# Key norms and T's products ahead of the Gram products, wider scan gaps, and later constants, adds and loads in the first layer

## The chip, the cores and the metric

The kernel runs on one core of a Trainium2 chip. The metric is the device time of one execution in microseconds (us). TensorE (PE) does the matrix products, VectorE (DVE), ScalarE (ACT) and GpSimd (POOL) the elementwise work, and SyncE (SP), ACT and POOL issue DMAs from their instruction queues. Each queue runs in the order in which it was written.

## The reference, cut to what matters

Two residual layers on x of 512 tokens by 2048 channels, all in float32.

```
layer 0: out = diff_attention(rms_norm(x)), 8 heads, w_in 2048 x 8192, w_out 2048 x 2048
         a = softmax(q1 k1) - lam * softmax(q2 k2);  o = rms_norm(a v) * silu(gate);  x += o @ w_out
layer 1: out = rwkv7(rms_norm(x)), 32 heads of 64, w_in 2048 x (4*2048 + 192), w_out 2048 x 2048
         p = token-shifted h @ w_in -> r, k, v, g, and decay w, rate a from a low-rank part
         kk = k / max(|k|, 1e-12) per head
         scan over t:  S = S * w_t + (S a_t) b_t + v_t k_t,   y_t = S r_t     (a = -kk, b = kk * a)
         y = group_norm(y) ... * silu(g);  x += y @ w_out
```

The scan of layer 1 is done in chunks of 64 tokens: the Gram products of the keys and receptances within a chunk, an inverse T of a triangular matrix made from them and from the key norms |k|, and then a short chain of small products from chunk to chunk.

## The kernel before, in words

**Precision and projections.** A float32 operand is split into a rounded high part and the rest (`split_w`: ACT casts `wh` on L105, DVE subtracts for `wl` on L106), and a product is three matmuls, high by high, high by low, low by high (`mm3`). A weight group of 512 KB (tile `wraw`) is loaded, split by ACT and DVE, and used by 128x512 matmuls. All these projections are the main stream of PE (tile `pp`, L122 and L567).

**Chains.** Work that isn't a projection is threaded into this stream by hand. `Chain` is a generator whose `yield n` says after how many more projection matmuls its next step is issued. `tick` is called after each projection matmul and counts down the *first* chain of the list only; the next chain begins to count when the first has ended. `finish` issues all remaining steps of a chain at once. `issue_after` and `high_priority` set what an instruction is ordered behind within its queue.

**First layer.** Eight heads, one after the other; `unit_head` (L540 on) makes q, k, v and gate of a head with sums of halves of the weights: three of four weight blocks are loaded, used, and then changed in place by an accumulating DMA that POOL issues (`add_w`, L86), in tiles `Ta` to `Td` and `wraw`. Head h's projections carry the attention of head h-1 as a chain (start 56 ticks in, 20 for head 1). In the `h == 1` turn the constants of the second layer (`rwkv_consts`: three DMAs on ACT, then on DVE 2 + 10 + 8 small operations, L1164 to L1171, from tile `pb`) are made as a chain with `yield 10` and `yield 8`; as it was appended before the attention chain of head 1 is, that chain stands behind it. In the last head, `third()` loads the weights of block (2,2) (`b22`) with the load ordered behind the last matmul of product S2, and the add straight behind the load. After the heads, rows `hH`, `hL` of the attention output are read back by SP (L931), and `new_x` (L945) loads x for the residual: column blocks 0 and 1 from POOL's queue, 2 and 3 from SP's.

**Second layer.** A loop over 16 pairs of heads, j = 0 to 15. One turn has four projections (k, r, v, gate) of 48 matmuls each, 192 ticks. In turn j:

- `chain(j-1)` is begun: `t_combine` loads the inverse's blocks into `TT`, waits 10 ticks, transposes on DVE (`T1`, L1382; a profile row calls it T), waits 8, makes T's products (tile `px`, L1388), waits 19, the second products (L1398), waits 8; then `scan_pair`, eight chunks of three steps: `sm<-VS,G` (L1469), `sm<-rhs,TT` (L1480), `sm<-VS,BKT` (L1487), with `gap` ticks after the first and second and `gap_s` after the third. Between them ACT copies `rhs` (L1472) and `VS` (L1482), and DVE makes the next `VS` (L1491). Gaps are (6, 7) at j = 3 and (6, 8) for j = 4 to 14. After the last chunk come the outputs `Y` (L1509 and L1513, both buffers of PSUM bank `pc`) and `centre` on DVE (L1524 to L1526), which frees them.
- 18 ticks into the v projection, `behind` finishes the chain of pair j-2, if it hasn't ended, and issues `gram(j)`: 32 Gram products `gp` (L1290; first half in bank `pb`, second half in bank `pc`), and right behind them one step of the running chain, T's products. Then come four ACT copies to `G`, the key norms (two `pt<-sHx` / `pt<-sLx` matmuls, L1209 and L1210, in bank `pb`), the ACT copy `ssl` (L1302), and DMAs on SP that write norms (`ltd<-ssl`) and Gram blocks (`ltd<-G`, L1310) to DRAM.
- `t_solve` reads them back (`LT<-ltd`, four DMAs on POOL, L1344) and solves for T on DVE (`tmpl`, `Tm`, L1346 to L1358). The result goes through DRAM to the next turn's `TT`.

Of the kernel before, what the change touches and what calls it, by code (L numbers as in the profile page):

```python
# [13 lines left out]
F32 = mybir.dt.float32  # L14
# [9 lines left out]
P = 128  # L24
D = 2048
T = 512
# [56 lines left out]
def add_w(g, raw, part, k0):  # L83

    w, c = part
    g.nc.gpsimd.dma_start(out=raw[:], in_=w[c][:, k0 : k0 + KG], accum_op=ALU.add)  # L86


@urgent
# [441 lines left out]
def unit_head(g, aps, h, t1s, sq, turned):  # L531


    nc = g.nc
    c1, c2 = qk_cols(aps, h), vg_cols(aps, h)
    acc1 = g.work.tile([P, 2, 512], F32, name="acc1", tag="acc1", bufs=1)
    acc = [None, None, acc1[:, 0], acc1[:, 1]]
    q = [t[:] for t in t1s]
    N = NH4 // KG
    last = h == NH - 1  # L540

    def pair():
        return [g.pp.tile([P, 512], F32, name="pp", tag="pp") for _ in range(2)]

    def load(i, k0, parts):
        pool, tag, bufs = (g.work, "Te", 1) if i == N - 1 else (g.wraw, "wraw", 3)
        raw = pool.tile([P, KG, 512], F32, name="wraw", tag=tag, bufs=bufs)
        load_w(g, raw, parts, k0 + i * KG, slice(0, KG))
        return raw

    def split(raw):
        return split_w(g, None, KG, 512, 0, raw)

    def block(k0, t0):
        return lambda k, t: [x[k0 + k][:, t0 + t * P : t0 + (t + 1) * P] for x in (g.hH, g.hL)]

    def form(nm, i):
        return lambda k, t: [x[:, t * P : (t + 1) * P] for x in g.sums[nm][i * KG + k]]

    def products(out, lhs, raw, start=False, end=False):  # L560
        wt = split(raw)
        for t in range(2):
            first = start
            for lo in range(2):
                for k in range(KG):
                    for x in lhs(k, t)[: 2 - lo]:
                        m = nc.tensor.matmul(out[t][:], x, wt[lo][:, k, :], start=first, stop=end and lo == 1 and k == KG - 1,  # L567
                                             skip_group_check=True)
                        tick(g, m)
                        first = False  # L570

    def all_groups(out, lhs, raw, start=False, end=False, then=None):
        for i in range(N):
            r = raw(i)
            products(out, lhs(i), r, start and i == 0, end and i == N - 1)
            if then:
                add_w(g, r, then[0], then[1] + i * KG)

    def s4(out, keep, start=False, end=False):
        def raw(i):  # L580
            keep.append(load(i, NH4, c2))
            return keep[-1]
        all_groups(out, lambda i: form("S4", i), raw, start, end, None if last else (c2, 0))

    chained = lambda i: g.Ts[i]
    y = pair()
    all_groups(y, lambda i: block(NH4 + i * KG, 0), lambda i: load(i, NH4, c1), True, True)
    copy_out(g, q[:2], y)
    y = pair()
    all_groups(y, lambda i: block(i * KG, 0), chained, True, False, (c2, 0))  # L590
    take(g, q[:2], y)
    X = pair()
    all_groups(X, lambda i: form("S1", i), chained, True, last, (c2, NH4))
    copy_out(g, acc[2:], X)
    b22 = []
    if not last:
        s4(X, b22, end=True)
        G, acc[:2] = gates(g)
        copy_out(g, acc[:2], X)
    all_groups(y, lambda i: form("S2", i), chained, then=(c1, NH4))  # L600
    behind = g.m.ins
    if last:
        G, acc[:2] = gates(g)
    take(g, acc[:2], y, ALU.subtract, acc[2:] if last else None)

    def square():
        X = pair()
        all_groups(X, lambda i: block(NH4 + i * KG, 256), chained, True, True)
        return X

    def third():
        for i in range(N):
            if last:
                with g.tc.issue_after(behind):
                    b22.append(load(i, NH4, c2))
                add_w(g, b22[i], c2, i * KG)
            products(y, form("S3", i), b22[i], end=i == N - 1)
        take(g, acc[2:], y, ALU.subtract)

    head_qk(g, t1s, sq, [0, 1])  # L620
    if last:
        copy_out(g, q[2:], square())
        third()
        take(g, q[2:], y)
        head_qk(g, t1s, sq, [2, 3])
        turned()
        X = pair()
        s4(X, [], True, True)
        take(g, acc[:2], X)
        return head_vg(g, h, acc, G)  # L630
    turned()
    third()
    copy_out(g, q[2:], y)
    values = head_vg(g, h, acc, G)
    X = square()
    first_tiles(g, aps, h + 1)
    take(g, q[2:], X)
    head_qk(g, t1s, sq, [2, 3])
    return values
# [156 lines left out]
def layer0(g, aps):  # L796
# [3 lines left out]
    with ExitStack() as cx:  # L800
# [91 lines left out]
        for h in range(NH):  # L892
# [11 lines left out]

            rest = [(g, t1s, *qkT, t) for t in (2, 3)]
            if h:
                values = unit_head(g, aps, h, t1s, sq, lambda: Chain(g, keys(2), 9))
            else:
                for ts in ([0, 1], [2, 3]):
                    head_qk(g, t1s, sq, ts)  # L910
                Chain(g, keys(2), 120)
                input_sums(g, pairs, False)
                ps = unit_tok(g, g.hH, g.hL, vg_cols(aps, h), 512)
                acc1 = g.work.tile([P, 2, 512], F32, name="acc1", tag="acc1", bufs=1)
                G, vg = gates(g)
                vg += [acc1[:, 0], acc1[:, 1]]
                copy_out(g, vg, ps)
                for c in list(g.chains):
                    c.finish(g)
                input_sums(g, pairs, True)  # L920
                first_tiles(g, aps, 1)
                values = head_vg(g, h, vg, G)
            before = qkT + (sq,) + values
            if h == 1:
                Chain(g, rwkv_consts(g, aps))
                g.chains[0].step(g)
        rows = []
        for k in range(KT - 2):
            rows.append([g.hp.tile([P, T], F32R, name=n, tag=n) for n in ("hH", "hL")])
            for x, d in zip(rows[k], g.ys):  # L930
                nc.sync.dma_start(out=x[:].bitcast(F32), in_=d[k * P : (k + 1) * P, :])  # L931
        ch = Chain(g, attention(g, h, *before, 20, rows, rest), 16)

        def all_rows(n, _):
# [6 lines left out]

        def new_x(cb):
            xq = g.work.tile([P, NT, 512], F32, name="xq", tag=("sA", "sB", "qkL", "qkT")[cb], bufs=1)
            for t in range(NT):
                (nc.gpsimd if cb < 2 else nc.sync).dma_start(out=xq[:, t, :], in_=aps["x"][0, t * P : (t + 1) * P, cb * 512 : cb * 512 + 512])  # L945
            xs.append(xq)
            return xq

# [330 lines left out]
def gram(g, j, p, before):  # L1279

    nc, w, BK = g.nc, g.work, p.BK
    p.G = w.tile([P, NC_, 2, 2, C], F32, name="G1", tag="G1", bufs=2)
    p.BKT = w.tile([P, NC_, P], F32, name="BKT", tag="BKT", bufs=2)
    halves = []
# [10 lines left out]
    for c0, gp in halves:  # L1295
        for h in range(2):
            nc.scalar.copy(p.G[:, c0 : c0 + 4, :, h, :], gp[h][:].rearrange("p (u x t) -> p u x t", u=4, x=2))
    ps = g.ps.tile([P, 512], F32, name="pt", tag="pb", bufs=2)
    sum_channels(g, ps[:2, :], g.ones[:, 0 : P : C], p.k2)
    ss = w.tile([2, T], F32, name="ssl", tag="thg", bufs=1)  # L1300
    with g.tc.high_priority(offset=SOLVE if j == D // P - 1 else 0):
        nc.scalar.copy(ss[:], ps[:2, :])  # L1302
        for half in range(2):
            nc.sync.dma_start(
                out=g.ltd[j % 2, half, :, :, HALF, :],
                in_=ss[:].rearrange("h (c b t) -> h c b t", c=NC_, b=2)[:, :, half, :])
        for half in range(2):
            for h in range(2):
                q0 = h * C + half * HALF
# [53 lines left out]
GAP_D, GAP_X, GAP_T = 18, 19, 8  # L1363


def t_combine(g, j, p):

    nc, w, TT = g.nc, g.work, g.TT[j % 2]
    for h in range(2):
# [5 lines left out]
    T1 = w.tile([P, NC_, HALF], F32, name="T1", tag="T1", bufs=1)  # L1375
    X = w.tile([P, NC_, HALF], F32, name="X", tag="X", bufs=1)
    px = g.ps.tile([P, 512], F32, name="px", tag="pd", bufs=1)
    yield GAP_D - GAP_T
    for h in range(2):
        r_ = slice(h * C, h * C + C)  # L1380
        with g.tc.issue_after(g.centred) if g.centred else ExitStack():
# [64 lines left out]
HEADS = ((0, slice(0, C)), (1, slice(C, P)))  # L1446


def chain(g, j, p, delay, gap, gap_s, others=()):
    def steps():  # L1450
        yield from t_combine(g, j, p)
        yield from scan_pair(g, j, p, gap, gap_s, dict(others))

    p.chain = Chain(g, steps(), delay)
    return p.chain
# [97 lines left out]
def layer1(g, aps):  # L1553
    nc, tc = g.nc, g.tc
    with ExitStack() as cx:
# [22 lines left out]
        for j in range(D // P):  # L1578
            p = pairs[j]
            if j:  # L1580
# [2 lines left out]
                if j > 1:  # L1583
                    others.append((3, lambda i=j - 2: finish_y(g, i, pairs[i])))
                full = LAG <= j < D // P - 1
                gaps = (6, 8 if j > LAG else 7) if full else (4, 5) if j > 1 else (3, 4)
                chain(g, j - 1, pairs[j - 1], 5, *gaps, others).step(g)
                if j == 1:
                    pairs[0].chain.wait += 34
            stage2(g, j, r, p)  # L1590

            def behind(m, j=j, p=p):
                if j > 1:
                    pairs[j - 2].chain.finish(g)
                with tc.issue_after(m.ins):
                    gram(g, j, p, j > 2 and pairs[j - 1].chain)
                p.rfs = split_act(g, p.rf[:], w, "x")
                if j == 2:
                    pairs[1].chain.wait = 16
# [160 lines left out]
```

## Time and profile before

| what | us |
|---|---|
| median of 3 runs | 2133.65 (2128.92 to 2135.13) |
| the profiled execution | 2131.0 |
| its span in the trace | 2129.3 |
| PE busy in the span | 2091.2 |
| one turn of the second layer, start of `gp` to start of `gp` (1379.27 to 1441.18) | 61.91 |

All stretches below are in us from the start of the span. A row of the time line has the start, the duration, the engine and line, the operation with its output and inputs, and in brackets the idle time of the engine before it with what ended that. A row of the windows has, for one stretch, its length, the busy time of PE, PE's weight loads, DVE, ACT and POOL with numbers of instructions, then the TensorE clock that was granted, as a share of full speed, the busy share of the DMA engines and GB/s. Rows of the waits have total, number and longest.

### The profile page before, as it was taken

The page shows a single profiled execution, that of the slowest core. Times are in us where ns is not written, and L with a number is a line of the kernel's source. Part 1 is how long each engine was busy: PE and PEld are TensorE (multiplying, and loading weights), DVE is VectorE, ACT ScalarE, POOL GpSimd, SP SyncE. Part 2 cuts the span into 40 slices and gives each one's busy share as a digit, 9 for nine tenths or more (in the row PEclk, how much of TensorE's full clock was granted, in tenths as well). Part 3 has the DMA queues.
Part 4 walks back from the last instruction along what each step waited for, and adds up shares of the span by engine and source line. Part 5 has one row for each costly group of instructions (what it writes and reads, how often), then busy time and mean ns, then how long its engine had stood idle before and what let it go on. Part 6 is the DMA issues. An engine that isn't in the chain of part 4 may idle for free.

```text
span 2129.3 us, 34082 instructions
## 1 busy us (share of the span) xinstructions
PE 2091.2 (98%) x11852; PEld 1690.3 (79%) x11852; DVE 1613.0 (76%) x4129; ACT 1155.5 (54%) x2278; POOL 367.9 (17%) x735
## 2 busy tenths in 40 slices
PE   9999999999999999999999999999999999999999
PEld 7888788888887788878677877778777777877787
DVE  6987888888888875576677777887777788776645
ACT  5765556566565543355555555555555555545322
POOL 1021111102113000101222221222222122231101
PEclk9999999999999999999999999999999999999999
DMA  8587878879789936722222332332333333345565
GB/s 266 161 166 186 161 167 186 164 189 172 178 183 215 314 113 179 150 90 88 78 74 84 98 91 84 93 91 77 94 103 88 84 91 92 107 134 178 173 171 121
DMA packets 158972, 294.60 MB, mean 138 GB/s; under 512 B 64352, under 2 KB 81760, under 8 KB 158800
## 3 DMA queue, kind: packets, MB, share of 16 engines
q1 hardware_dynamic: 109696, 182.82, 27.7%
q0 software_dynamic: 24448, 85.64, 22.0%
q10 hardware_dynamic: 24656, 23.97, 3.4%
q8 instruction: 93, 1.52, 0.3%
q14 instruction: 79, 0.65, 0.1%
HBM read 268.71 MB, written 23.66 MB: 137 GB/s over the span
## 4 chain that ended last, share of the span: by engine, by line
PE 77%; DVE 10%; ACT 6%; issue 3%; DMA 3%; ACTq 0%; POOL 0%; SPq 0%; DVEq 0%; POOLq 0%
PE pp L122 36%; PE pp L567 21%; PE pt L122 4%; DVE wl L106 3%; ACT wh L105 1%; PE gp L1290 1%; PE sc L122 1%; PE sm L1480 1%; PE sm L1469 1%; PE sm L1487 1%; PE o L122 1%; DVE tmpl L1355 1%; ACT VS L1427 1%; PE lora L122 1%; PE z L122 1%
## 5 line engine op out<-in xcount | busy, mean ns | idle before, releaser
L106 DVE TENSOR_TENSOR wl<-wraw,wh 128x1024 fp32r<-128x1024 f32 (+2 forms) x291 | 360.4, 1239 | 257.5 <-ACT wh L105 249.7
L105 ACT CAST wh<-wraw 128x1024 fp32r<-128x1024 f32 (+2 forms) x291 | 303.8, 1044 | 296.9 <-PE pp L122 130.3
L122 PE MATMUL pp<-hH,wl 128*128 128x512 f32 x1024 | 415.1, 405 | 0.0
L122 PE MATMUL pp<-hH,wh 128*128 128x512 f32 x1024 | 414.4, 405 | 0.0
L122 PE MATMUL pp<-hL,wh 128*128 128x512 f32 x1024 | 413.1, 403 | 0.0
L122 PEld LDWEIGHTS pp<-hH,wh 128*128 128x128 f32 x1024 | 193.7, 189 | 34.7 <-issue 0.6
L122 PEld LDWEIGHTS pp<-hL,wh 128*128 128x128 f32 x1024 | 193.9, 189 | 34.4
L122 PEld LDWEIGHTS pp<-hH,wl 128*128 128x128 f32 x1024 | 193.8, 189 | 34.0
L567 PE MATMUL pp<-wh,hH 128*128 128x512 f32 x448 | 177.8, 397 | 0.8 <-DVE G L528 0.8
L567 PE MATMUL pp<-wh,hL 128*128 128x512 f32 x448 | 176.8, 395 | 0.0
L122 PE MATMUL pp<-wh,hH 128*128 128x512 f32 x372 | 145.8, 392 | 3.9 <-ACT hH L1091 1.6
L122 PE MATMUL pp<-wl,hH 128*128 128x512 f32 x372 | 146.3, 393 | 0.4 <-DVE wl L106 0.4
L122 PE MATMUL pp<-wh,hL 128*128 128x512 f32 x372 | 146.0, 393 | 0.3 <-DVE hL L1092 0.2
L1355 DVE SCALAR_TENSOR_TENSOR tmpl<-LT,Tm 128x60 f32<-128x60 f32 (+24 forms) x496 | 134.7, 272 | 12.1
L567 PE MATMUL pp<-wl,hH 128*128 128x512 f32 x448 | 141.2, 394 | 1.3 <-DVE wl L106 1.3
L1475 POOL COPY SA<-VS 64x64 f32<-64x64 f32 x224 | 57.7, 257 | 466.6 <-DVE VS L1491 399.8
L1357 DVE TENSOR_TENSOR Tm<-Tm,tmpl 128x60 f32<-128x60 f32 (+24 forms) x496 | 103.6, 209 | 10.0 <-DVE tmpl L1355 0.2
L1472 ACT COPY rhs<-sm 64x64 f32<-64x64 f32 x256 | 53.0, 207 | 99.9 <-PE sm L1469 97.4
L567 PEld LDWEIGHTS pp<-wl,hH 128*128 128x128 f32 x448 | 84.8, 190 | 19.4 <-DVE wl L106 2.1
L567 PEld LDWEIGHTS pp<-wh,hH 128*128 128x128 f32 x448 | 84.7, 189 | 18.6 <-DVE G L528 1.2
L567 PEld LDWEIGHTS pp<-wh,hL 128*128 128x128 f32 x448 | 84.8, 189 | 16.4
L122 PEld LDWEIGHTS pp<-wh,hH 128*128 128x128 f32 x372 | 69.9, 188 | 19.6 <-ACT hH L1091 2.6
(393 smaller groups left out, 4426.5 us busy)
## 6 DMA issues: line engine op xcount, KB each, us to landing
wraw<-in_rw_w_in_dram SPq DMA_DIRECT2D x128, 512.0 KB, 3.9
wraw<-in_da_w_in_dram SPq DMA_DIRECT2D x75, 512.0 KB, 3.5
wraw<-in_da_w_in_dram POOLq DMA_DIRECT2D x28, 512.0 KB, 6.1
wraw<-in_da_w_out_dram SPq DMA_DIRECT2D x26, 512.0 KB, 4.5
wraw<-in_rw_w_out_dram SPq DMA_DIRECT2D x26, 512.0 KB, 4.5
Ta<-in_da_w_in_dram POOLq DMA_DIRECT2D x21, 512.0 KB, 5.9
Tb<-in_da_w_in_dram POOLq DMA_DIRECT2D x21, 512.0 KB, 5.8
Tc<-in_da_w_in_dram POOLq DMA_DIRECT2D x21, 512.0 KB, 5.8
```

The source lines that it names most:

```text
L105: a = nc.scalar.copy(hi[:, ks], raw[:, ks])
L106: d = nc.vector.tensor_sub(lo[:, ks], raw[:, ks], hi[:, ks].bitcast(F32))
L122: m = nc.tensor.matmul(out, a, b, start=s, stop=e, skip_group_check=skip)
L567: m = nc.tensor.matmul(out[t][:], x, wt[lo][:, k, :], start=first, stop=end and lo == 1 and k == KG - 1, skip_group_check=True)
L1290: m = nc.tensor.matmul(gp[h][:, i * P : (i + 1) * P], BK[r_, c0 + i, :, :], p.AR[r_, c0 + i, :, :], start=True, stop=True)
L1355: nc.vector.scalar_tensor_tensor(tt, LT[:, i : i + 1, i + 1 :].to_broadcast([P, s, n]), n2[:, i : i + 1], Tm[:, 0:s, i : i + 1].to_broadca ...
L1357: nc.vector.tensor_add(Tm[:, 0:s, i + 1 :], Tm[:, 0:s, i + 1 :], tt)
L1427: nc.scalar.copy(p.VS[(1 - h) * C : (2 - h) * C, par : NC_ : 2, h, :], pv[par * C : par * C + C, :, h, :])
L1469: nc.tensor.matmul(sm[:, 0:P], both(p.G[:, c, 0]), both(VS[:, c]), start=True, stop=True)
L1472: nc.scalar.copy(rhs[r_, :], sm[r_, h * C : h * C + C])
L1475: nc.gpsimd.tensor_copy(p.SA[r_, c - 1, :], VS[r_, c, h, :])
L1480: nc.tensor.matmul(sm[:, P : P + C], both(g.TT[j % 2][:, c]), rhs[:], start=True, stop=True)
```

## The change

1. **Gram.** The key norms (two matmuls, `ssl` copy, `ltd<-ssl` DMAs) stand ahead of the Gram products, in bank `pa` (one buffer, that of the scan's `sm`), and their copy and DMAs always at the priority of the solve.
2. **T's products and gaps.** For j = 4 to 14 the wait ahead of the transposes is 4 ticks in place of 10, gram no longer issues a step of the chain behind its products, and the gaps are (7, 8) in place of (6, 8).
3. **Constants.** In the turn h == 1 of the first layer, `rwkv_consts` is issued at once and isn't a chain.
4. **Last head.** The loads of block (2,2) aren't ordered any more; their adds are ordered behind the last add of the earlier products. The chain of keys starts after 16 ticks, not 9.
5. **x loads.** All four column blocks go through SP's queue, behind the last row load of `hH`, `hL`.

```diff
-    g.nc.gpsimd.dma_start(out=raw[:], in_=w[c][:, k0 : k0 + KG], accum_op=ALU.add)
+    return g.nc.gpsimd.dma_start(out=raw[:], in_=w[c][:, k0 : k0 + KG], accum_op=ALU.add).ins
...
-                add_w(g, r, then[0], then[1] + i * KG)
+                g.added = add_w(g, r, then[0], then[1] + i * KG)
...
-    behind = g.m.ins
...
-                with g.tc.issue_after(behind):
-                    b22.append(load(i, NH4, c2))
-                add_w(g, b22[i], c2, i * KG)
+                b22.append(load(i, NH4, c2))
+                with g.tc.issue_after(g.added):
+                    add_w(g, b22[i], c2, i * KG)
...
-                values = unit_head(g, aps, h, t1s, sq, lambda: Chain(g, keys(2), 9))
+                values = unit_head(g, aps, h, t1s, sq, lambda: Chain(g, keys(2), 9 if h < NH - 1 else 16))
...
-                Chain(g, rwkv_consts(g, aps))
-                g.chains[0].step(g)
+                for _ in rwkv_consts(g, aps):
+                    pass
...
-                nc.sync.dma_start(out=x[:].bitcast(F32), in_=d[k * P : (k + 1) * P, :])
+                loaded = nc.sync.dma_start(out=x[:].bitcast(F32), in_=d[k * P : (k + 1) * P, :]).ins
...
-            for t in range(NT):
-                (nc.gpsimd if cb < 2 else nc.sync).dma_start(out=xq[:, t, :], in_=aps["x"][0, t * P : (t + 1) * P, cb * 512 : cb * 512 + 512])
+            with tc.issue_after(loaded):
+                for t in range(NT):
+                    nc.sync.dma_start(out=xq[:, t, :], in_=aps["x"][0, t * P : (t + 1) * P, cb * 512 : cb * 512 + 512])
...
 def gram(g, j, p, before):
+    ps = g.ps.tile([P, 512], F32, name="pt", tag="pa", bufs=1)
+    sum_channels(g, ps[:2, :], g.ones[:, 0 : P : C], p.k2)
+    ss = w.tile([2, T], F32, name="ssl", tag="thg", bufs=1)
+    with g.tc.high_priority(offset=SOLVE):
+        nc.scalar.copy(ss[:], ps[:2, :])
+        for half in range(2):
+            nc.sync.dma_start(out=g.ltd[j % 2, half, :, :, HALF, :], ...
...
-    ps = g.ps.tile([P, 512], F32, name="pt", tag="pb", bufs=2)
-    sum_channels(g, ps[:2, :], g.ones[:, 0 : P : C], p.k2)
-    ss = w.tile([2, T], F32, name="ssl", tag="thg", bufs=1)
     with g.tc.high_priority(offset=SOLVE if j == D // P - 1 else 0):
-        nc.scalar.copy(ss[:], ps[:2, :])
-        for half in range(2):
-            nc.sync.dma_start(out=g.ltd[j % 2, half, :, :, HALF, :], ...
...
-def t_combine(g, j, p):
+def t_combine(g, j, p, lead):
-    yield GAP_D - GAP_T
+    yield lead
...
-                gaps = (6, 8 if j > LAG else 7) if full else (4, 5) if j > 1 else (3, 4)
-                chain(g, j - 1, pairs[j - 1], 5, *gaps, others).step(g)
+                early = full and j > LAG
+                gaps = (7, 8) if early else (6, 7) if full else (4, 5) if j > 1 else (3, 4)
+                chain(g, j - 1, pairs[j - 1], 5, *gaps, others, 4 if early else GAP_D - GAP_T).step(g)
...
-                    gram(g, j, p, j > 2 and pairs[j - 1].chain)
+                    gram(g, j, p, j > 2 and not early and pairs[j - 1].chain)
```

More of the change, by code (lines that the diff above doesn't have):

```diff
@@ L1281, in gram @@
     nc, w, BK = g.nc, g.work, p.BK
+    ps = g.ps.tile([P, 512], F32, name="pt", tag="pa", bufs=1)
[4 more added lines that the diff above has]
+        for half in range(2):
+            nc.sync.dma_start(
+                out=g.ltd[j % 2, half, :, :, HALF, :],
+                in_=ss[:].rearrange("h (c b t) -> h c b t", c=NC_, b=2)[:, :, half, :])
     p.G = w.tile([P, NC_, 2, 2, C], F32, name="G1", tag="G1", bufs=2)
@@ L1297, in gram @@
             nc.scalar.copy(p.G[:, c0 : c0 + 4, :, h, :], gp[h][:].rearrange("p (u x t) -> p u x t", u=4, x=2))
-    ps = g.ps.tile([P, 512], F32, name="pt", tag="pb", bufs=2)
-    sum_channels(g, ps[:2, :], g.ones[:, 0 : P : C], p.k2)
-    ss = w.tile([2, T], F32, name="ssl", tag="thg", bufs=1)
     with g.tc.high_priority(offset=SOLVE if j == D // P - 1 else 0):
-        nc.scalar.copy(ss[:], ps[:2, :])
-        for half in range(2):
-            nc.sync.dma_start(
-                out=g.ltd[j % 2, half, :, :, HALF, :],
-                in_=ss[:].rearrange("h (c b t) -> h c b t", c=NC_, b=2)[:, :, half, :])
         for half in range(2):
@@ L1446, with chain @@
 HEADS = ((0, slice(0, C)), (1, slice(C, P)))
-def chain(g, j, p, delay, gap, gap_s, others=()):
+def chain(g, j, p, delay, gap, gap_s, others=(), lead=GAP_D - GAP_T):
     def steps():
-        yield from t_combine(g, j, p)
+        yield from t_combine(g, j, p, lead)
         yield from scan_pair(g, j, p, gap, gap_s, dict(others))
@@ L1590, in layer1, with behind @@
             stage2(g, j, r, p)
-            def behind(m, j=j, p=p):
+            def behind(m, j=j, p=p, early=j and early):
                 if j > 1:
```

## The prediction

> **What bounds the kernel now.** I read the page first, then PE's waits, the windows around each long wait, and the time line at those places.
>
> ```profile
> PE 2091.2 (98%) x11852; PEld 1690.3 (79%) x11852; DVE 1613.0 (76%) x4129; ACT 1155.5 (54%) x2278; POOL 367.9 (17%) x735
> ```
>
> The page's line of busy times reads as one bottleneck: TensorE is busy in all but 38 us of the 2129.3 us span, and no edit takes a projection matmul away. What can be won is PE's waits and the time in which its clock is low; what can be lost is new waits. So the waits of PE come next (waited for: total, times, longest).
>
> ```profile
> PE sm L1480 <- ACT rhs L1472: 4.7, 12, 0.7
> PE yt L391 <- DVE y L382: 3.9, 2, 3.4
> PE px L1388 <- DVE T L1382: 3.3, 2, 3.2
> PE sm L1487 <- ACT VS L1482: 2.1, 11, 0.2
> PE px L1388 <- DVE y L1550: 1.6, 1, 1.6
> ```
>
> Two are single long waits, one in a head of the first layer and one at the start of the second layer's loop; two are small ones in nearly each turn. The windows show what the clock did behind the long ones (the column before the last two is the granted clock).
>
> ```profile
> 258.00:262.00 4.00, 3.21 (x8) 2.32 (x9) 3.86 (x16) 3.40 (x8) 0.00 (x0) 0.50 0.52 177
> 262.00:266.00 4.00, 4.00 (x15) 3.08 (x15) 1.09 (x6) 1.89 (x4) 0.00 (x0) 0.67 0.00 0
> 350.00:440.00 90.00, 89.95 (x430) 74.26 (x430) 78.20 (x204) 54.95 (x98) 13.63 (x16) 1.00 0.82 178
> 660.00:706.00 46.00, 43.03 (x210) 33.84 (x208) 36.16 (x116) 24.52 (x47) 12.18 (x17) 1.00 1.01 227
> 1031.00:1035.00 4.00, 3.91 (x37) 2.89 (x38) 0.48 (x2) 1.65 (x2) 2.85 (x5) 0.70 1.03 255
> 1035.00:1041.00 6.00, 6.00 (x48) 4.74 (x47) 1.23 (x1) 2.08 (x6) 0.00 (x0) 0.50 0.37 108
> 1041.00:1045.00 4.00, 4.00 (x19) 3.37 (x19) 1.06 (x5) 1.42 (x5) 0.61 (x3) 0.77 0.00 0
> 1314.00:1376.00 62.00, 61.40 (x428) 49.11 (x421) 47.39 (x131) 35.06 (x78) 13.49 (x31) 1.00 0.31 90
> 1940.00:1943.00 3.00, 1.89 (x36) 1.72 (x37) 3.00 (x5) 2.61 (x5) 0.00 (x0) 1.00 0.96 300
> ```
>
> Behind the 3.4 and the 3.2 us wait the clock is half for some microseconds; behind the 1.6 us wait (1940 to 1943) it stays at 1.00. A wait of that length costs more than itself, a shorter one only itself.
>
> **Constants outside the chains (edit 3).** In before the constants' chain stands ahead of the attention of head 1 and holds it 10 + 8 ticks back; and its DVE operations come in one block.
>
> ```profile
> 199.73 0.17 DVE L1164 TENSOR_SCALAR prm_hw<-pb 128x16 f32<-128x16 f32 x1 [0.24 <-DMA pb<-in_rw_cols_dram]
> 201.99 1.23 DVE L106 TENSOR_TENSOR wl<-Tb,wh 128x1024 fp32r<-128x1024 f32 x1
> 203.27 0.74 PE L567 MATMUL pp<-wl,hH 128*128 128x512 f32 x2 [0.88 <-DVE wl L106]
> 257.94 0.69 PE L391 MATMUL yt<-ident,y 128*128 128x128 f32 x2 [3.44 <-DVE y L382]
> 259.42 0.79 PE L567 MATMUL pp<-wh,hH 128*128 128x512 f32 x1 [0.79 <-DVE G L528]
> ```
>
> The block holds DVE from 199.73 to 201.99, so `wl` is late and PE waits 0.88; the late attention makes PE wait 3.44 and then 0.79. The half clock costs half of the 3.21 us busy in the first window and 0.33 x 4 in the second, 2.9. Sum: 0.88 + 3.44 + 0.79 + 2.9 = **8.0 us**. In the changed order head 2's chain starts as those of the heads behind it, and a head without the constants ahead of it runs clean (350 to 440: 89.95 of 90 busy), so I take all 8.0. The constants' operations remain, but three of them only stand ahead of that `wl`, and the others between later splits; if their cover is gone they cost the same 0.88 again. Ends: 4 (the wait gone, the clock not) and 8.9.
>
> **Norms first, at j = 0 and 1 (edit 1).** The long `px` wait is for T of pair 0.
>
> ```profile
> 981.52 0.43 SPq L1310 DMA_DIRECT2D ltd<-G  x1
> 985.16 2.03 POOL L1344 DMA_DIRECT2D LT<-ltd  x4 [5.15 <-DMA ltd<-G]
> 992.48 1.23 DVE L106 TENSOR_TENSOR wl<-wraw,wh 128x1024 fp32r<-128x1024 f32 x1 [4.92 <-ACT wh L105]
> 993.62 0.17 DVE L1346 TENSOR_SCALAR LT<-LT 128x32 f32<-128x32 f32 x1
> 994.74 0.25 DVE L1355 SCALAR_TENSOR_TENSOR tmpl<-LT,Tm 128x30 f32<-128x30 f32 x1
> 1022.73 1.22 DVE L106 TENSOR_TENSOR wl<-wraw,wh 128x1024 fp32r<-128x1024 f32 x1
> 1030.60 0.44 DVE L1382 STREAM_TRANSPOSE T<-TT 64x256 f32<-64x256 f32 x1 [3.40 <-DMA TT<-td]
> 1031.09 0.69 PE L1388 MATMUL px<-T,G 32*32 32x32 f32 x16 [3.17 <-DVE T L1382]
> ```
>
> On SP's queue the last Gram write (981.52) stood behind two norm writes that waited for their copy; in the changed order the four stand together behind the norms, and the read-back on POOL can go some 2 us sooner. DVE gains less than that read-back, since the `wl` at 992.48 waits on its own input. Two orders change on DVE: the solve's first five operations (993.62 to 994.99, 1.4 us) now stand ahead of that `wl`, and the solve's last one ahead of the `wl` at 1022.73 (1.2). So T comes 2.6 us earlier; PE is 0.5 earlier too, as the norms fill an idle stretch ahead of the Gram products. The wait becomes 3.17 - 2.6 + 0.5 = 1.1, below the 1.6 that left the clock alone, and the half clock (0.30 x 4 + 0.50 x 6 + 0.23 x 4 = 5.1) goes. **7.2 us**; ends: 0 (nothing earlier) and 8.3 (no wait left).
> By the Trainium skill (TensorE: Matmul & The Clock Gate, section "HAM oscillation — how this bites in real kernels") the clock is cut for idle gaps of more than about 3.4 us, the length of one activity window. By that rule a 3.17 us wait wouldn't cut it, something else would have, and this term would be 2.1; the trace speaks against a limit as sharp as that, and bears the rule out at 3.44.
>
> **The forced end of a chain (edit 2).** A turn has 192 ticks. In before a chain is 10 + 8 + 19 + 8 ticks and eight chunks of 6 + 6 + 8 less the last 8, 197 in all; it hands 5 back since gram issues T's products early, and so it ends before gram comes. After, it is 4 + 8 + 19 + 8 + 8 x 22 - 8 = 207, with nothing handed back, in turns of 192. So it runs over. At j = 4 T's products do come ahead of the Gram products. At j = 5 the outputs, and from j = 6 to 15 the last scan step, the last TT product and the outputs are issued back to back at tick 18 by `finish`; the next chain starts only then, and T's products land 12 projection matmuls *behind* the Gram products. The trace has one such forced end, at j = 3:
>
> ```profile
> 1125.88 0.38 PE L1469 MATMUL sm<-VS,G 128*128 128x128 f32 x2
> 1128.27 0.68 PE L1513 MATMUL Y<-SA,AR 64*64 64x64 f32 x28
> 1128.88 1.16 PE L1290 MATMUL gp<-AR,BK 64*128 64x128 f32 x16
> 1130.75 1.88 PE L1290 MATMUL gp<-AR,BK 64*128 64x128 f32 x16 [0.71 <-DVE Tm L1357]
> 1132.56 0.40 PE L1209 MATMUL pt<-sHx,ones 128*2 128x512 f32 x1
> 974.49 2.06 PE L1290 MATMUL gp<-AR,BK 64*128 64x128 f32 x32
> 1984.97 1.20 PE L1509 MATMUL Y<-VS,G 128*64 128x64 f32 x32
> 1986.10 0.68 PE L1513 MATMUL Y<-SA,AR 64*64 64x64 f32 x28
> ```
>
> The 32 Gram matmuls took 1128.88 to 1132.56, 3.7 us, against 2.0 (974.49, of which the last 0.1 overlaps): the second half needs the two buffers of bank `pc`, which DVE's `centre` frees one after the other, so 1.7 are lost. In the changed order the two norm matmuls (0.5) stand in between and cover part: 1.2. From the scan step to the end of the outputs it took 3.0; without waits it is 1.1 + 0.6 for the outputs (1984.97, 1986.10) and some 0.7 for scan step, TT product and one projection, 2.4. So 0.6 is waiting for `rhs` and `VS`, and about 0.1 more where no projection stands between. Per turn 1.9, ten turns 19, and 1.2 at j = 5: **+20 us**. Ends: half of it (10, if DVE is quicker where no solve is mixed in) and 2.6 a turn (27). At j = 3 itself the norms save 0.5: **-0.4**.
>
> **The wider gaps (edit 2).** They aim at the small waits inside a turn.
>
> ```profile
> 1410.83 0.40 PE L122 MATMUL pp<-hH,wl 128*128 128x512 f32 x1
> 1411.57 0.43 PE L1480 MATMUL sm<-rhs,TT 128*128 128x64 f32 x2 [0.34 <-ACT rhs L1472]
> ```
>
> The steady window 1314 to 1376 has 0.6 us without PE. The rows of idle time are short of the true loss: here the start comes 0.74 behind the last one where 0.23 is the pace, so 0.51 is lost and 0.34 is listed. 0.6 x 1.5 = 0.9, some 1.0 a turn. One more projection is 0.23 us for each step; ACT's queue in the changed order mostly has its long operations behind the copies at these places. For 11 chains (j = 4 to 14) I take 1.0 each, **-10**; ends 0 and -15.
>
> **Last head and x loads (edits 4, 5).**
>
> ```profile
> 662.07 1.05 ACT L105 CAST wh<-Ta 128x1024 fp32r<-128x1024 f32 x1 [2.36 <-DMA Ta<-in_da_w_in_dram]
> 667.03 1.05 ACT L105 CAST wh<-Tb 128x1024 fp32r<-128x1024 f32 x1 [3.43 <-DMA Tb<-in_da_w_in_dram]
> ```
>
> From 660 to 706 the DMA engines are full (1.01) and PE lacks 3.0 of 46, in part because splits wait for adds into `Ta`, `Tb`. Block (2,2)'s four adds stood ahead of these on POOL's queue; they go behind them, and 2 MB of x leave this stretch. I take half, **-1.5**; ends -3 and +1 (the four adds now late for the third product). The x loads land behind 740 us on an emptier queue; nothing needs them before.
>
> The end of the loop: the last chain ends 8 ticks later, so the 1.6 us wait of `px` for `y` goes and the wait of what follows its outputs grows as much: 0, ends -1.6 and +1.6.
>
> **Sum.** -8.0 - 7.2 - 0.4 + 20 - 10 - 1.5 = -7.1. The profiled execution took 2131.0, so 2123.9 in its terms. The median of the runs shown is 2.65 above it: **2126.5**. A measurement of this kernel tells about 0.3% (6.4 us) from no change.
>
> **Rivals.**
> *The forced end is cheap and the gaps pay in full.* For: the one sample has solve operations mixed into `centre`, the later turns don't. Then +10 and -14: 2112.5; halfway, 2117.
> *T isn't ready earlier.* For: DVE stands on `wl` and on a DMA round trip, not on LT alone. Then 7.2 stay: 2133.7.
> *The half clock at 1031 has another cause*, the many 32x32 products there, which PE counts as little work. For: the windows hold them. Against: the same products stand in all turns at 1.00. Then 5.1 stay: 2131.6. This is what the page's rule would give.
> *Slower: the wait chain at tick 18.* `rhs` waits behind a 1.05 us cast on ACT, and `centre` behind another DVE operation, in each of ten turns: 2.6 a turn, while the interior waits only move. +27, 0: 2143.5. It decides from a net 1.7 a turn on, where the loop eats the 17 that the rest brings. Against: the interior waits are at steps that the gaps do widen.
> *Head 2 isn't cleared* (the change doesn't do what it says): the attention's own DVE work is late, or the block of constants only moves: 7 of 8 stay, 2133.5. Against: the heads behind it.
>
> **How the numbers follow.** Forecast 0.42 (its own range 2120 to 2133), cheap end 0.28, T late 0.07, clock 0.05, slower 0.12, head 2 0.06. The range 2112 to 2139 reaches from the full cheap case to half of the slower one. Faster by over 0.3% (below 2127.3): 0.25 of the forecast and 0.27 of the cheap end, 0.52; within 0.3%: 0.17, 0.01, 0.06, 0.05 and 0.05, 0.34; slower: 0.12 and 0.02, 0.14.
>
> **What would show it.** Head 2: no wait at `yt` and no clock below 1.00 near 260. j = 1: a `px` wait of about 1 us with clock 1.00 behind it. Turns 6 to 15: a wait of `sm` for `rhs`, the second half of `gp` 0.9 to 1.4 late, `px` behind 12 projections, and a turn of about 62.8 instead of 61.9, with the `rhs` and `VS` waits inside it gone. I'd be wrong if the turn isn't longer than 61.9, or if it is longer than 63.6.

## The result, and the profile after

The changed kernel takes **2149.49 us** (median, 2148.39 to 2151.01) beside 2132.14 for the kernel before: ratio 1.0082 (95% interval 1.0064 to 1.0100), 17 us slower where 7 us faster was forecast. The profiled execution took 2148.67 us.

```profile
span 2147.0 us, 34067 instructions
PE 2100.5 (98%) x11852; PEld 1705.5 (79%) x11852; DVE 1617.1 (75%) x4129; ACT 1154.7 (54%) x2278; POOL 387.6 (18%) x727
```

TensorE has the same 11852 instructions and 9 us more of busy time. (A waiting group counts partly as busy: the second half of `gp` is the example below.) The Gram products are one mark per turn, so the first question is in which stretch the 17.7 us of the two spans arise. The starts of `gp` in both traces give it:

| stretch | before | after | difference |
|---|---|---|---|
| start to first Gram (turn 0) | 974.49 | 967.30 | -7.2 |
| Gram 0 to Gram 5 | 280.9 | 280.2 | -0.7 |
| Gram 5 to Gram 15, ten turns | 619.1 (61.9 each) | 642.3 (64.2 each) | +23.1 |
| Gram 15 to the end | 254.8 | 257.2 | +2.4 |

The stretch up to the first Gram products gained 7.2 of the 9.5 that the constants and the last head were to bring (8.0 and 1.5); the loop took back three times as much. The rows that answer to those of before, PE's waits in the whole span (total, times, longest):

```profile
PE sm L1481 <- ACT rhs L1473: 10.6, 23, 0.7
PE gp L1299 <- DVE s L1526: 6.6, 12, 0.6
PE pp L122 <- DVE wl L106: 3.3, 3, 2.2
PE px L1389 <- DVE T L1383: 2.2, 1, 2.2
PE px L1389 <- DVE y L1413: 1.9, 1, 1.9
PE sm L1488 <- ACT VS L1483: 1.1, 3, 0.4
PE yt L391 <- DVE y L382: 0.4, 1, 0.4
```

The 3.4 us wait of `yt` in head 2 is gone. The waits for `rhs`, which the wider gaps were to take away, have more than doubled (4.7 before), and a wait of the Gram products, 12 times, is new. One turn's boundary on PE's time line shows both it and the forced steps:

```profile
1436.79 0.39 PE L1470 MATMUL sm<-VS,G 128*128 128x128 f32 x2
1437.10 0.68 PE L1510 MATMUL Y<-VS,G 128*64 128x64 f32 x12
1437.74 0.43 PE L1481 MATMUL sm<-rhs,TT 128*128 128x64 f32 x2
1439.02 0.68 PE L1514 MATMUL Y<-SA,AR 64*64 64x64 f32 x28
1439.63 0.39 PE L1209 MATMUL pt<-sHx,ones 128*2 128x512 f32 x1
1440.18 1.16 PE L1299 MATMUL gp<-AR,BK 64*128 64x128 f32 x16
1441.92 1.66 PE L1299 MATMUL gp<-AR,BK 64*128 64x128 f32 x16 [0.58 <-DVE s L1526]
1443.51 0.50 PE L122 MATMUL pp<-hH,wh 128*128 128x512 f32 x1
1446.48 1.09 PE L1389 MATMUL px<-T,G 32*32 32x32 f32 x32
```

Scan step, TT product and outputs stand with no projection between them; the Gram products take from 1440.18 to 1443.51, 3.3 us instead of 2.0; T's products (`px`) come 3 us behind the Gram products, not ahead of them. On DVE the `centre` of these outputs has an operation of another kind in its way, `sLx`, ahead of the two `yc` that free the buffers:

```profile
1440.75 0.69 DVE L1101 TENSOR_TENSOR sLx<-mixr,sHx 128x512 fp32r<-128x512 f32 x1
1441.36 0.42 DVE L1527 TENSOR_TENSOR yc<-Y,s 128x256 f32<-128x256 f32 x1
1441.89 0.42 DVE L1527 TENSOR_TENSOR yc<-Y,s 128x256 f32<-128x256 f32 x1
```

The second half of `gp` begins 0.14 behind the end of the first `yc`.

The first pair and the second (start, duration, operation, idle before), and the clock around them (the column before the last two):

```profile
1022.33 1.09 PE L1389 MATMUL px<-T,G 32*32 32x32 f32 x32 [1.91 <-DVE y L1413]
1077.30 0.69 PE L1389 MATMUL px<-T,G 32*32 32x32 f32 x16 [2.18 <-DVE T L1383]
```

```profile
1022.00:1026.00 4.00, 3.67 (x71) 3.04 (x71) 0.27 (x1) 3.12 (x6) 1.95 (x4) 1.00 0.51 143
1079.00:1083.00 4.00, 4.00 (x49) 3.04 (x48) 0.00 (x0) 1.34 (x3) 0.00 (x0) 0.57 0.11 36
1083.00:1087.00 4.00, 4.00 (x21) 3.37 (x19) 0.66 (x2) 2.18 (x5) 0.00 (x0) 0.58 0.00 0
```

The wait at pair 0 shrank from 3.17 to 1.91 and the clock behind it stays full, but pair 1 now has a wait of 2.18 with the clock at 0.57 behind it, where before had neither. From Gram 0 to Gram 2 the changed kernel is 5.6 us quicker, and from Gram 2 to 3 it is 5.1 slower. What the 1.91 is for isn't T any more:

```profile
1020.01 0.44 DVE L1383 STREAM_TRANSPOSE T<-TT 64x256 f32<-64x256 f32 x1 [1.76 <-DMA TT<-td]
1021.58 0.69 DVE L1413 TENSOR_TENSOR y<-pt,mixv 128x512 f32<-128x512 f32 x1
```

The first part of T is there at 1020.45, just as PE comes to `px`. But `px` lies in bank `pd`, which has one buffer, and in it stands the `pt` that `y` reads. In before `y` ran ahead of T on DVE (1026.51, T at 1030.60); now both transposes stand ahead of it, and `px` starts when `y` is done.

### The profile page after: what moved, and what is told of

Read it like the earlier page. It is cut to its first block, busy times and chain, and to the rows that moved or that the text cites. A ratio compares the mean times of both kernels' runs of the same rounds, so it can differ in the third digit from the quotient of the medians.

```text
span 2147.0 us, 34067 instructions
## 1 busy us (share of the span) xinstructions
PE 2100.5 (98%) x11852; PEld 1705.5 (79%) x11852; DVE 1617.1 (75%) x4129; ACT 1154.7 (54%) x2278; POOL 387.6 (18%) x727
## 5 line engine op out<-in xcount | busy, mean ns | idle before, releaser
L106 DVE TENSOR_TENSOR wl<-wraw,wh 128x1024 fp32r<-128x1024 f32 (+2 forms) x291 | 354.9, 1220 | 189.1 <-ACT wh L105 180.3
L1476 POOL COPY SA<-VS 64x64 f32<-64x64 f32 x224 | 65.9, 294 | 576.8 <-DVE VS L1492 424.4
L567 PEld LDWEIGHTS pp<-wh,hH 128*128 128x128 f32 x448 | 84.2, 188 | 20.3 <-ACT wh L105 3.1
L1483 ACT COPY VS<-sm 64x64 f32<-64x64 f32 x256 | 52.7, 206 | 65.6 <-PE sm L1481 59.4
```

What stands on the lines that cost most here:

```text
L106: d = nc.vector.tensor_sub(lo[:, ks], raw[:, ks], hi[:, ks].bitcast(F32))
L1476: nc.gpsimd.tensor_copy(p.SA[r_, c - 1, :], VS[r_, c, h, :])
L1483: nc.scalar.copy(VS[r_, c, h, :], sm[r_, P : P + C])
```

## The experiments

**Theory 1**: the chain is longer than its turn, and what is forced at tick 18 costs some 2.3 us in each of ten turns. **Rival**: the new order itself, norms or T's products ahead of the Gram products, lengthens the turn. Two kernels undo part of the loop, two do one part of the first layer alone.

*The loop as before, all else as changed.*

```diff
-                gaps = (7, 8) if early else (6, 7) if full else (4, 5) if j > 1 else (3, 4)
-                chain(..., others, 4 if early else GAP_D - GAP_T).step(g)
+                gaps = (6, 8 if early else 7) if full else (4, 5) if j > 1 else (3, 4)
+                chain(..., others).step(g)
...
-                    gram(g, j, p, j > 2 and not early and pairs[j - 1].chain)
+                    gram(g, j, p, j > 2 and pairs[j - 1].chain)
```

> The changed kernel with the loop's lead, gaps and the step behind the Gram products as before; norms first, constants, adds and x loads as changed. Theory (the chain that overruns its turn costs 2.33 us in each of turns 6 to 15, and the tail's new wait of 2.2 us with half clock belongs to it too): turns back to 61.9, so 23.3 to 26 us less than the changed kernel, 2124 to 2127. Rival (norms ahead of the Gram products are what lengthens the turn): turns stay near 64, above 2145.

Measured 2121.64, ratio to before 0.9943 (0.9921 to 0.9964). The ten turns are 61.56 us. That is 28 us below the changed kernel, a little more than the theory had. One part of the theory failed: the stretch behind Gram 15 still takes 256.5, with a wait of `px` for `y` of 2.4 us and a half clock, so the tail's 2.4 doesn't belong to edit 2. The whole loss is in edit 2, and the rest of the change beats the kernel before. The rival falls for the norms: with them ahead a turn is 0.35 *shorter* than before's 61.91.

*Gaps (6, 8), the rest as changed.*

```diff
-                gaps = (7, 8) if early else (6, 7) if full else (4, 5) if j > 1 else (3, 4)
+                gaps = (6, 8 if early else 7) if full else (4, 5) if j > 1 else (3, 4)
```

> The changed kernel with gaps (6, 8) in place of (7, 8) for j = 4 to 14; the lead of 4 ticks and gram without a step of the chain stay. The chain is then 191 ticks in a turn of 192, so nothing is forced and T's products do stand ahead of the Gram products. Theory (the overrun costs): turn 61.9, total 2124 to 2128. Rival (T's products ahead of the Gram products, or the short lead, cost by themselves): turn 62.5 or more, total above 2131.

Measured 2127.34, ratio 0.9970 (0.9960 to 0.9980). Now nothing is forced and T's products stand ahead of the Gram products in nearly every turn, and 22 us come back. The total is the theory's, the turn isn't: the ten turns are 62.35 on average, 0.8 above the old loop's, near the rival's 62.5. They aren't alike. A chain of 191 ticks in a turn of 192 slides by one tick a turn, and the turns take from 61.5 to 63.3, the longest where `px` falls among the Gram products. PE's waits in turns 5 to 15 of this kernel,

```profile
PE sm L1488 <- ACT VS L1483: 3.8, 10, 0.9
PE sm L1470 <- DVE VS L1492: 2.0, 6, 0.6
PE sm L1481 <- ACT rhs L1473: 0.4, 1, 0.4
```

and in the same turns of the kernel with the old loop:

```profile
PE sm L1481 <- ACT rhs L1473: 3.9, 11, 0.4
```

The steps stand at other ticks, and other copies are late: `VS` in place of `rhs`.

*Constants alone, on the kernel before.*

```diff
-                Chain(g, rwkv_consts(g, aps))
-                g.chains[0].step(g)
+                for _ in rwkv_consts(g, aps):
+                    pass
```

> The kernel before with the constants outside the chains and nothing else. Theory: the waits of 0.88, 3.44 and 0.79 us and the half clock near 260 go, 8.0 us less than before. Rival (part of the 7.2 us by which the changed kernel reaches the first Gram products earlier comes from the last head): 4 to 6 less.

Measured 2126.03, ratio 0.9970 (0.9956 to 0.9984): 6.7 us less, between theory and rival; the interval reaches from 3 to 9, so the theory's 8.0 isn't excluded. The 3.4 us wait of `yt` and the waits beside it are gone.

*Last head and x loads alone, on the kernel before* (edits 4 and 5, whole).

```diff
-                with g.tc.issue_after(behind):
-                    b22.append(load(i, NH4, c2))
-                add_w(g, b22[i], c2, i * KG)
+                b22.append(load(i, NH4, c2))
+                with g.tc.issue_after(g.added):
+                    add_w(g, b22[i], c2, i * KG)
...
-                (nc.gpsimd if cb < 2 else nc.sync).dma_start(out=xq[:, t, :], ...
+                    nc.sync.dma_start(out=xq[:, t, :], ...      # under issue_after(loaded)
```

> The kernel before with the last head's loads and adds, its later chain of keys, and the x loads as changed, and nothing else. Theory: the waits for the adds go and others of the same size come between 690 and 710, within 1 us of before. Rival (the step as forecast): 1.5 us less.

Measured 2133.87, ratio 1.0001 (0.9986 to 1.0016): no difference, but the interval is 3 us to either side and doesn't tell the theory from the rival. The waits for splits near 668 and 673 are gone, and PE's time line has four further on, 2.1 us in all:

```profile
702.11 0.50 PE L567 MATMUL pp<-wh,hH 128*128 128x512 f32 x1 [0.55 <-ACT wh L105]
703.83 0.73 PE L567 MATMUL pp<-wl,hH 128*128 128x512 f32 x2 [0.52 <-DVE wl L106]
707.50 0.44 PE L391 MATMUL yt<-ident,y 128*128 128x128 f32 x2 [0.44 <-DVE y L382]
712.93 0.50 PE L567 MATMUL pp<-wh,hH 128*128 128x512 f32 x1 [0.62 <-ACT wh L105]
```

They aren't all new. Between 655 and 730 PE's waits were 3.3 us in before, four of them behind 690, so the trace has the stretch some 1.2 us better, near the forecast's 1.5. Nor are they for block (2,2)'s adds, which had landed by 709.3, the first of them at 698.9, 6.6 us ahead of its cast at 705.51.

**Theory 2**: the overrun costs 1.9 a turn, as forecast, and the seventh tick of the gap gives nothing. **Rivals**: the gap pays and the overrun costs more, or the gap costs.

*The overrun with gaps of 6.* The chain is made 207 ticks long in another way.

```diff
-    yield GAP_X
+    yield GAP_X + more          # more = 16 for j = 4 to 14
...
-                gaps = (7, 8) if early else ...
+                gaps = (6, 8 if early else 7) if full else ...
```

> The changed kernel with gaps (6, 8) but 16 ticks more between T's two products for j = 4 to 14, so that the chain is 207 ticks long as in the changed kernel and the same three steps are forced at tick 18. It differs from the changed kernel in the inner gap alone, and from the kernel with gaps (6, 8) in the overrun alone. Theory (the overrun costs 1.9 us a turn, the seventh tick of a gap nothing either way): turn 64.0 to 64.4, total 2147 to 2150. Rival (a wider gap does pay 1.0 a turn, and the overrun costs more than 1.9): turn 65.2, total 2159. Other rival (a wider gap costs): turn 63.5 or less, total below 2143.

Measured 2152.72, ratio 1.0080 (1.0065 to 1.0095); the turn is 64.48. Against the kernel with gaps (6, 8) and no overrun that is **+2.1 a turn**; against the changed kernel (64.23) the seventh tick gives **0.25 a turn**, where 1.0 was forecast. (Counted from the old loop's 61.56 it is 2.9.) Where the waits went is seen in PE's waits of turns 5 to 15 of this kernel,

```profile
PE sm L1488 <- ACT VS L1483: 10.7, 10, 1.1
PE gp L1299 <- DVE s L1526: 5.7, 10, 0.6
PE sm L1481 <- ACT rhs L1473: 3.8, 10, 0.4
```

and of the changed one:

```profile
PE sm L1481 <- ACT rhs L1473: 9.3, 20, 0.7
PE gp L1299 <- DVE s L1526: 5.2, 9, 0.6
```

The wait at `gp` is the same; inside the turn the large wait is for another copy. In the changed kernel it is this one, on PE and on ACT:

```profile
1488.70 0.46 PE L1470 MATMUL sm<-VS,G 128*128 128x128 f32 x2
1491.47 0.43 PE L1481 MATMUL sm<-rhs,TT 128*128 128x64 f32 x2 [0.70 <-ACT rhs L1473]
```

```profile
1489.31 0.73 ACT L1259 ACTIVATE k<-mixk,prm_kk 128x512 f32<-128x512 f32 x1 [0.27 <-DVE mixv L1436]
1489.94 1.03 ACT L105 CAST wh<-wraw 128x1024 fp32r<-128x1024 f32 x1
1491.00 0.20 ACT L1473 COPY rhs<-sm 64x64 f32<-64x64 f32 x1
```

`sm` began at 1488.70; its copy to `rhs` stood on ACT's queue behind 1.7 us of other work and began at 1491.00. Seven projections of 0.23 us don't cover that, nor would eight.

*Gaps (7, 7), a lead of 3, and the step behind the Gram products, so that nothing is forced.*

```diff
-                gaps = (7, 8) if early else (6, 7) if full else (4, 5) if j > 1 else (3, 4)
-                chain(..., others, 4 if early else GAP_D - GAP_T).step(g)
+                gaps = (7, 7) if early else (6, 7) if full else (4, 5) if j > 1 else (3, 4)
+                chain(..., others, 3 if early else GAP_D - GAP_T).step(g)
...
-                    gram(g, j, p, j > 2 and not early and pairs[j - 1].chain)
+                    gram(g, j, p, j > 2 and pairs[j - 1].chain)
```

> The changed kernel with gaps (7, 7), a lead of 3 ticks and the step behind the Gram products, for j = 4 to 14: 199 ticks, handed back so that the chain ends ahead of gram and nothing is forced, and T's products stand ahead of the Gram products. Theory (the waits inside a turn only move when the gap is one wider): turn 61.5 to 62.3, as with gaps of 6. Rival (the wider gap pays, the overrun hid it): turn 60.5 to 61.

Measured 2115.96 (2114.00 to 2123.36), ratio 0.9915 (0.9894 to 0.9937); the turn is 61.58. Gaps (7, 7) without an overrun give the turn of gaps (6, 8) in the old loop, as the theory had it. That isn't the price of the seventh tick alone, since the gap after the third step is one tick narrower here, and the largest wait now stands there, ahead of `sm<-VS,G`:

```profile
PE sm L1470 <- DVE VS L1492: 9.7, 10, 1.0
PE sm L1488 <- ACT VS L1483: 3.0, 10, 0.3
```

*Norms first alone, on the kernel before* (edit 1, whole).

```diff
 def gram(g, j, p, before):
+    ps = g.ps.tile([P, 512], F32, name="pt", tag="pa", bufs=1)
+    sum_channels(g, ps[:2, :], g.ones[:, 0 : P : C], p.k2)
...
-    ps = g.ps.tile([P, 512], F32, name="pt", tag="pb", bufs=2)
-    sum_channels(g, ps[:2, :], g.ones[:, 0 : P : C], p.k2)
```

> The kernel before with the key norms ahead of the Gram products and nothing else. Theory (worth the difference between the kernel with the old loop and that with the constants alone): 4 to 5 us less than before, of which 0.4 a turn from turn 5 on; the long wait for T at the first pair shrinks to about 2 us without a half clock, and a wait of above 2 us with a half clock comes at the second pair. Rival (the gain is the first pair's alone): turn 61.9 and 7 us less up to the second pair.

Measured 2127.34, ratio 0.9964 (0.9950 to 0.9978). In its trace Gram 0 to Gram 2 takes 94.9 us instead of 100.7, Gram 2 to 3 takes 59.0 instead of 53.7, and the turns from 5 on 61.5. So the gain at the first pair is lent to the second, as the theory says, and what stays is 0.4 a turn, some 4 us. The runs gained about 8, more than the 4 to 5 expected; the one trace, 1.6 us shorter than that of before, doesn't place the rest.

*The banks of the two Gram halves exchanged, in the changed kernel.*

```diff
-    for c0, tag in ((0, "pb"), (4, "pc")):
+    for c0, tag in ((0, "pc"), (4, "pb")):
```

> The changed kernel with the banks of the two halves of the Gram products exchanged, so that the first half needs the bank that the outputs' buffers hold. Theory (the wait in the Gram products is for the centring that frees that bank): the cover of the first half, 1.0 us, goes; turn 65.2, total 2158 to 2160. Rival (the Gram products wait for their operands): no change, 2149.

Measured 2148.78, ratio 1.0060 (1.0045 to 1.0076), turn 64.24: no change, the outcome that was written for the rival. PE's time line has the same shape as in the changed kernel, with the first half without a wait:

```profile
1437.03 1.16 PE L1299 MATMUL gp<-AR,BK 64*128 64x128 f32 x16
1438.77 1.66 PE L1299 MATMUL gp<-AR,BK 64*128 64x128 f32 x16 [0.58 <-DVE s L1526]
```

The second half waits for `centre` again, and `centre` frees only the buffers of `pc`. So the half in `pb` will have been put first again, and the edit didn't make the order that it was meant to try; that is inferred, as the rows don't name a bank. The run doesn't decide. So another:

*The chain's end still forced at tick 18, norms and Gram products at tick 30.*

```diff
-            if n == 1 and 3 * kk + 3 == behind[0]:
-                behind[1](m)
+            for b in (behind[:2], behind[2:]):
+                if n == 1 and b and 3 * kk + 3 == b[0]:
+                    b[1](m)
...
-            def behind(m, j=j, p=p, early=j and early):
+            def ended(m, j=j):
                 if j > 1:
                     pairs[j - 2].chain.finish(g)
+
+            def behind(m, j=j, p=p, early=j and early):
...
-            stage_v(g, j, p, proj(2, j, behind=(18, behind)))
+            stage_v(g, j, p, proj(2, j, behind=(18, ended, 30 if j and early else 18, behind)))
```

> The changed kernel with the end of the chain still forced at tick 18, but norms and Gram products only at tick 30 for j = 4 to 14, so that twelve projection matmuls (2.8 us) stand between the outputs and the Gram products, and T's products come just ahead of these. Theory (of the 2.2 us that the overrun costs a turn some 1.3 are the wait for the bank that the centring frees, the rest the waits for rhs and VS): turn 62.9 to 63.2, total 2136 to 2140. Rival (most of it are the rhs and VS waits of the forced steps and of the turn): turn 63.8 or more, total 2145 or more.

Measured 2138.49, ratio 1.0023 (1.0008 to 1.0038); the turns 6 to 14 are 63.0. The Gram products run through:

```profile
1435.95 2.06 PE L1300 MATMUL gp<-AR,BK 64*128 64x128 f32 x32
```

The turn is 1.2 shorter than the changed kernel's 64.23, and the Gram products alone 1.3. So the wait for the bank is some 1.2 of what the overrun costs a turn. The twelve projections would also cover a wait for operands that come late, but the row names `centre`. T's products come at another place here too, and the waits inside the turn are for `VS` now.

*The two kernels that beat both, again in more rounds* (their diffs are above: gaps (7, 7), and the loop as before).

> Again the changed kernel with gaps (7, 7), lead 3 and the step behind the Gram products, in more rounds. Theory: 0.6 to 1.0% below the kernel before; against the kernel with the old loop, within 0.3%, since their turns are the same 61.5 to 61.6 and only the end differs. Rival: the 5 us between their medians stay.

> Again the changed kernel with the loop's lead, gaps and step as before, in more rounds, beside the kernel with gaps (7, 7) on the same chip. Theory: 0.4 to 0.7% below the kernel before, within 0.3% of the kernel with gaps (7, 7). Rival: the 5 us between their medians stay.

Measured 2120.81, ratio 0.9943 (0.9931 to 0.9956), and 2123.39, ratio 0.9958 (0.9944 to 0.9972). Both beat both kernels, and the 5.7 us between their first medians shrank to 2.6, or 0.1%. The second is within its theory, the first just short of it (0.57% where 0.6 to 1.0 was expected). Their intervals overlap, so these runs don't tell which is better; by their ratios they are some 12 and 9 us below the kernel before.

## Why the prediction was wrong, point by point

The sum failed in edit 2: in the entry for the gaps, and in the new order of T's products, which had none. The overrun itself was priced nearly right.

- **The wider gaps (-10).** This step failed. "Some 1.0 a turn" was taken as won; with the overrun the tick was worth 0.25, and no run shows more. The working took a wait of 0.51 and set against it one projection of 0.23, and trusted that the other 0.28 would go because ACT's long operations would stand elsewhere. They did, in front of other copies. The slower rival had said so ("the interior waits only move", chance 0.12), and the kernels with other gaps show it: the large wait is for `rhs`, or for `VS` on ACT, or for `VS` on DVE.
- **T's products ahead and the lead of 4 (costed at nothing).** The second step that failed. The kernel that has them without an overrun, with the old loop's gaps, takes 62.35 a turn against 61.56: +0.8. With gaps (7, 7) and a lead of 3, T's products stand ahead of the Gram products too and the turn is 61.58, so this isn't the order's own price. That it is again where the steps fall, in a chain that slides from turn to turn, is likely and wasn't tried.
- **The forced end (+20).** Right: 1.9 a turn forecast, 2.1 measured, 1.2 of it the bank (forecast 1.2). It was read off one forced end in the trace of before. The slower rival's `centre` behind another DVE operation is there too, the `sLx` above. The 2.1 is counted from the kernel with gaps (6, 8) and a lead of 4; counted from the old loop it is 2.9, the 0.8 being in it.
- **Constants (-8.0).** Right in mechanism; measured alone -6.7.
- **Norms at the first pair (-7.2).** The wait fell to 1.91 (forecast 1.1), and the half clock behind it went in this execution. T came sooner than forecast: 3.4 us (forecast 2.6), counted from the Gram products' start. What the step left out is what is late next, twice. At the first pair it is `y`, which DVE now does behind T. At the second, PE came 5.6 us sooner; the solve ended only some 1.5 sooner and T was transposed 1.2 later (counted from Gram 0), so 5.1 us went to a new wait of 2.18 and a new half clock. The limit of 1.6 us, below which a wait was to cost only itself, didn't hold: the last section has a 1.65 with a half clock. That the clock was full behind the 1.91 is luck. In the ten traces with norms first this wait is 1.75 to 2.01, and in four of them the clock fell behind it. The rival with another cause of the half clock isn't settled by that.
- **Norms in every turn (costed at nothing).** Worth -0.35 to -0.4 a turn from turn 5 on, some -4 in all. Not foreseen; how it comes about wasn't tried.
- **Last head (-1.5).** 0 within 3 us, so the runs neither bear it out nor refute it. The waits near 668 and 673 went, and the end of +1, late adds of block (2,2), didn't come.
- **The end of the loop (0).** +2.4 in the profiled executions. The 1.6 us wait for `y` went as forecast; a wait of 2.18 for `wl` at 1949.92 came, and the clock was at 0.50 behind it (1951 to 1953). But this stretch took 256.3 to 257.0 us in the three kernels that keep the gaps, the lead and T's products of before (constants, last head, norms alone), against 254.8 in before itself, so the 2.4 isn't shown to come from the change.

For a turn the terms are 61.91 - 0.35 (norms) + 0.8 (order and lead) + 2.1 (overrun) - 0.25 (gap) = 64.2, and 64.2 was measured. They close because each is the difference of two neighbouring kernels. In the forecast it was 61.9 + 1.9 - 1.0 = 62.8, with 63.6 named as the turn from which it is wrong. The 1.4 us between are 0.75 of the gap, 0.8 of order and lead and 0.2 of the overrun, less 0.35 of the norms; ten times, they are 14 of the 24.5 us by which the forecast missed. The second pair (5) is the largest of the rest; tail, last head and constants are each within what one kernel's runs or traces differ by. In the rivals, halfway between 2126.5 and 2112.5 is 2119.5, not 2117; nothing else hangs on it.

## What to carry to other kernels

A hand-made interleaving has a length: add up the ticks and compare with the turn before judging any spacing, since what doesn't fit is forced out together, here for 2.1 us a turn. A small wait behind an in-order queue need not be cured by one more slot; ask which long operation stands ahead of the copy, and expect it to stand ahead of another one after the move. When a stall goes, follow the same resource to its next use, here the bank that the stalled product writes and the next pair's solve, before the gain is booked.

## What the runs showed of the hardware

The granted clock fell behind waits much shorter than the 3.2 us of the trace of before, and not by their length alone. In the changed kernel a wait of 1.91 us left it at 1.00 and two of 2.18 us halved it. In the second execution of gaps (7, 7), at the same place as the 1.91, a wait of 1.82 us had it at 0.73 and 0.66:

```profile
1020.57 1.09 PE L1389 MATMUL px<-T,G 32*32 32x32 f32 x32 [1.82 <-DVE y L1413]
```

```profile
1021.00:1025.00 4.00, 4.00 (x63) 3.19 (x59) 0.00 (x0) 3.27 (x6) 1.24 (x3) 0.73 0.42 130
1025.00:1032.00 7.00, 7.00 (x29) 5.71 (x27) 1.76 (x3) 1.68 (x7) 0.23 (x1) 0.66 0.21 75
```

The 1.6 us wait of `px` for `y`, which left the clock at 1.00 in before, is 1.65 us in the kernel with the constants alone, and there the clock behind it is at 0.52:

```profile
1933.42 1.45 PE L1388 MATMUL px<-T,G 32*32 32x32 f32 x32 [1.65 <-DVE y L1550]
1934.00:1941.00 7.00, 7.00 (x35) 5.63 (x32) 5.33 (x10) 5.96 (x11) 0.00 (x0) 0.52 0.84 264
```

In the kernel with the banks exchanged a wait of 2.60 us left it at 1.00:

```profile
1947.36 0.50 PE L122 MATMUL pp<-hH,wl 128*128 128x512 f32 x1 [2.60 <-DVE wl L106]
1948.00:1956.00 8.00, 8.00 (x39) 6.63 (x38) 7.68 (x19) 5.41 (x10) 0.00 (x0) 1.00 0.60 167
```

And in the kernel with the overrun and gaps of 6 the clock was at 0.57 from 1081 to 1089, behind a wait of 1.04 us at 1079.08.

The stretch from Gram 1 to Gram 2 differs by 2.8 us between the second execution of gaps (7, 7) and the changed kernel for it (58.17 and 55.33); in the ten traces with norms first it is 55.2 to 58.3. By the Trainium skill (TensorE: Matmul & The Clock Gate, section "Part 1: The HAM clock gate (the "warmup" mystery)") the clock follows activity in a window that runs freely, so that the phase counts; these rows fit that, without showing the phase, and disagree with the 3.4 us of idle time that the page asks for. Such a place adds some 3 us of spread from run to run to this kernel.
